# The mixer's output projection by Strassen's seven products, with its residual input on the sync queue

## The chip, the cores and the metric

The kernel runs on one core of one Trainium2 chip. The metric is the device time of one execution in microseconds (us), the median of several runs. Engines: PE (TensorE, matrix products into PSUM banks), DVE (VectorE), ACT (ScalarE), POOL (GpSimd), and SP, which here only issues DMAs. A DMA can be issued by SP, ACT or POOL; each has its own queue, and in this kernel POOL's DMAs are the ones that add to what already stands in the target.

## The reference

One layer of a decoder trunk, 512 tokens by 1024 channels, all in float32. Cut to what matters here:

```python
y_a = pool_mixer(z_pool, w_pool[i], pool_scale[i]) @ w_branch_a[i]
y_b = spatial_gating(z_uv, sgu_norm[i], w_spatial[i], b_spatial[i]) @ w_branch_b[i]
x = x + (g_a * y_a + g_b * y_b) @ w_out[i]
h = rmsnorm(x, ffn_norm[i])
x = x + conv_ffn(h, w_up[i], conv_w[i], conv_b[i], w_down[i])
x = x + gate * (p[i] @ w_ple[i])
```

The change concerns the third line, a product of 512x1024 by 1024x1024, and the loads of `x` and `p` around it.

## The kernel before

**Products.** Every float32 operand is split into a high part (a cast to float32r) and a low part (the rest), and each product is three matmuls (`mm3`, L204 to L206): high by high, high by low, low by high. A matmul covers 128 rows of contraction and 512 columns.

**Weights.** They come in tiles of 128x1024 (512 KB). A list `todo` holds, in the order of use, a pair of functions for each tile: one that issues its load on SP (`load_raw`, L81; `fetch`, L105), one that splits it (`parts`: the high part by ACT at L68, `whi`; the low part by DVE at L69, `wlo`). `take()` hands the next split tile to the products and keeps two more split ahead (`AHEAD`) and up to four loaded behind those (`LOADS`). There are four buffers of split tiles and 37 buffers (`blk`) that raw tiles and activations share. Within these limits the framework's scheduler sets the order in which each engine's instructions stand; an engine then runs its own instructions strictly in that order.

**Seven products.** `seven()` computes a product of 512 tokens by Strassen's scheme, in halves of tokens, contraction and columns, with seven products instead of eight. The weights it needs are blocks a, b, c, d and sums of them. `plan_seven` makes the sums: with `adds="some"` mostly by DVE, with `adds="all"` all of them by POOL's adding DMAs (P5: b+a; P6: the same plus c, added in place after P5's split; P7: b+c; P4: P6's sum plus d, added in place after P6's split). On the activation side `combine` and `cut_into` build D, S2, S3 and E from the two halves. P1, P2 use one pair of PSUM banks, P5, P3 another, P6, P7, P4 the pair `seeded`. Between P6 and P7 ACT copies the `seeded` pair out (`copies(0)`, L368, tiles `u`), and P7 then goes on adding in that same pair. The input projections to v and to the gates run so, and so does the down projection, in three parts, the last with `adds="all"`.

**The stage of the change.** Branch A's projection runs by token (`by_token`): for each half `fh` of the columns, four weight tiles, for each tile 24 matmuls, into four banks. After each half DVE multiplies the banks by the gate and adds branch B (L578, L579; tiles `ga`, shown as `sg`). Then the result is turned: 8 times four 128x128 transposes on PE (L617), each time into one bank, split by ACT (L236) and DVE (L237). Then the output projection, again by token: 2 halves, 4 weight tiles each, 192 matmuls, drained by DVE into `x` (L629) with squares on ACT (L607) for the next norm. Then 24 matmuls of the embedding's input (`embed`), the norm (`rstd_1`, `xn` L652), and the turning for the FFN. The tokens' rows of x are loaded by ACT's queue (L584) and the embedding's input `pt` by ACT's queue too (L590), released by markers (`later`, a one-column copy) as soon as the first half of `ga[0]` stands; `pt` is split at once (`pp`).

Of the kernel before, what the change touches and what calls it, by code (L numbers as in the profile page):

```python
# [7 lines left out]
F32 = mybir.dt.float32  # L8
# [36 lines left out]
def trunk(ctx, tc, xT, xr, pT, wsT, par, bsp, w_u0, w_u1, w_v, w_ga, w_gb, w_p, w_pl,  # L45
# [38 lines left out]
    def pairs_of(n):  # L84

        return [(q, min(2, n - q)) for q in range(0, n, 2)]

    def plan(src, cols=CW, **kw):
        got = []
        todo.append((lambda: got.append(load_raw(src)), lambda: parts(got[0], cols, **kw)))  # L90

    def plan_seven(w, order=INNER, adds="vector", spare=(), q0=0, n=HK):

# [50 lines left out]

        return [unit(prod, ch) for prod in order for ch in pairs_of(n)]

# [33 lines left out]
    for i in range(KD):  # L180
        plan(w_a[i // 4, i % 4].rearrange(flat))
    for i in range(KD):
        plan(w_o[i // 4, i % 4].rearrange(flat))
    for k in range(2):
# [162 lines left out]

    def seven(op, drain, order=INNER, fill=()):


        fill = list(fill)
        n = len(op)
        bank_of = {}
# [19 lines left out]

        for prod in order:
            b, c = ops[prod]
            if b not in bank_of:
                bank_of[b] = seeded if b == "b" else [bank() for _ in range(2)]
            o = bank_of[b]
            first = b != "b" and b not in begun
            begun.add(b)  # L380
            for ch in pairs_of(n):
                step(o, c, take(), ch, first)
                if fill:
                    fill.pop(0)()
# [25 lines left out]

    def by_token(acts, fh, banks, kps, between=None):

        for kp in kps:
            c = take()
            for b in range(NT):
                for kk in range(2):
                    k = 2 * kp + kk
                    mm3(banks[b], act(acts[k], slice(b * P, (b + 1) * P)), wslice(c, kk, T), k == 0, k == KD - 1)


# [151 lines left out]


    for fh in range(2):
# [11 lines left out]
    pp = []  # L586
# [21 lines left out]

    def columns(z, b, f):

        return z[b][:, f // HK, f % HK * P:(f % HK + 1) * P]

    def turned(z, f):

        tp = bank()
        for b in range(NT):
            PE.transpose(tp[:, b * P:(b + 1) * P], columns(z, b, f), ident)  # L617
        return tp


    m = []
    for f in range(KD):
        m.append(split(turned(ga, f)))
    xss = [small.tile([P, 2], F32, tag="xss", name="xss", bufs=NT) for _ in range(NT)]
    for fh in range(2):
        banks = [bank() for _ in range(NT)] if fh == 0 else [*seeded, bank(), bank()]
        by_token(m, fh, banks, range(KD // 2))
        for b in range(NT):
# [167 lines left out]
def _layout(i):  # L796
# [9 lines left out]
    def th(w):  # L806
        return w.reshape(KD // 2, 2, P, 2, T).transpose(3, 0, 2, 1, 4)

    def sv(w):
        return w.reshape(2, HK, P, 2, T).transpose(0, 3, 1, 2, 4).reshape(4, HK, P, T)  # L810
# [8 lines left out]
    def pairs(z):  # L819
# [21 lines left out]
        "w_b": th(a["w_branch_b"][0]),  # L841
        "w_o": th(a["w_out"][0]),
        "w_up": pairs(up),

        "w_dn": a["w_down"][0].reshape(KF // 2, 2, P, 2, T).transpose(1, 3, 0, 2, 4).reshape(4, KF // 2, P, T),
        "w_g": a["w_ple_gate"][0].reshape(KD, P, D),
# [18 lines left out]
```

## Time and profile before

| what | value |
|---|---|
| median of 3 runs | 783.2 us (782.55 to 783.73) |
| the profiled execution, its own time | 781.51 us |
| its span in the trace | 779.8 us |
| busy: PE / DVE / ACT / POOL | 768.5 / 535.3 / 373.0 / 62.7 us |
| moved by DMA | 103.2 MB, mean 132 GB/s |
| branch A's second half, the turning, the output projection | from 292.77, 314.54, 319.07 us to 362.70 us |
| the embedding's 24 matmuls, the turning for the FFN | to 368.17 and 372.73 us |

The span is what the trace covers; the execution's own time is 1.7 us more. PE's busy time counts a matmul from its start to a modelled end, so PE's rate is read from the distance between starts, not from the duration. Times inside the trace are counted from the span's start.

### The profile page before, as it was taken

What the parts mean: (1) busy time and instruction counts of PE and PEld (TensorE: products, weight loads), DVE (VectorE), ACT (ScalarE), POOL (GpSimd) and SP (SyncE); (2) the same over time, 40 slices, a digit from 0 to 9 for tenths busy, and PEclk for the clock granted to TensorE, in tenths of its full rate; (3) what the DMA queues carried; (4) which work ended last, traced back from release to release, by engine and by line L of the source; (5) the groups of instructions that cost most, each with busy time, mean ns of one, the idle gap of its engine ahead of it and who ended that gap; (6) DMA issues with size and microseconds to landing.
All of it is one profiled execution on the core that took longest, in us unless ns stands there. A gap on an engine that the chain in (4) does not pass through costs nothing.

```text
span 779.8 us, 9304 instructions
## 1 busy us (share of the span) xinstructions
PE 768.5 (99%) x3482; PEld 636.9 (82%) x3482; DVE 535.3 (69%) x752; ACT 373.0 (48%) x538; POOL 62.7 (8%) x97
## 2 busy tenths in 40 slices
PE   9999999999999999999999999999999999999996
PEld 7888888888888888888788888888888888887785
DVE  7895688866576734635576768766677776777845
ACT  6576736582232312325545454534545435457823
POOL 2310200000112100001000000000001010030300
PEclk9999999999999999999999999999999999999998
DMA  8993625124032508101832344742336572384211
GB/s 329 324 240 109 163 78 194 54 98 170 31 114 75 216 24 315 67 0 47 331 111 51 96 118 98 278 141 54 82 107 136 189 192 78 109 171 112 82 55 54
DMA packets 40926, 103.21 MB, mean 132 GB/s; under 512 B 3633, under 2 KB 3761, under 8 KB 40881
## 3 DMA queue, kind: packets, MB, share of 16 engines
q1 hardware_dynamic: 33280, 86.78, 31.8%
q0 software_dynamic: 6016, 11.54, 9.0%
q10 hardware_dynamic: 1584, 4.31, 1.6%
q8 instruction: 27, 0.44, 0.2%
q14 instruction: 19, 0.15, 0.1%
HBM read 99.46 MB, written 3.15 MB: 132 GB/s over the span
## 4 chain that ended last, share of the span: by engine, by line
PE 82%; DVE 2%; ACT 1%; issue 1%; POOL 0%; POOLq 0%; DVEq 0%; ACTq 0%
PE mm L205 22%; PE mm L206 22%; PE mm L204 22%; PE sd L204 5%; PE sd L205 5%; PE sd L206 5%; DVE wlo L69 1%; PE mm L504 1%; PE mm L617 0%; DVE xn L652 0%; POOL fr L602 0%; PE mm L680 0%; ACT whi L68 0%; ACT sq L607 0%; DVE x L629 0%
## 5 line engine op out<-in xcount | busy, mean ns | idle before, releaser
L69 DVE TENSOR_TENSOR wlo<-raw,whi 128x1024 fp32r<-128x1024 f32 (+1 forms) x186 | 218.2, 1178 | 157.1 <-ACT whi L68 156.5
L68 ACT CAST whi<-raw 128x1024 fp32r<-128x1024 f32 (+1 forms) x179 | 184.0, 1031 | 204.9 <-PE mm L206 64.4
L205 PE MATMUL mm<-blk,whi 128*128 128x512 f32 x480 | 186.8, 389 | 0.0
L204 PE MATMUL mm<-blk,whi 128*128 128x512 f32 x480 | 186.8, 390 | 0.0
L206 PE MATMUL mm<-blk,wlo 128*128 128x512 f32 x480 | 186.6, 389 | 0.0
L204 PEld LDWEIGHTS mm<-blk,whi 128*128 128x128 f32 x480 | 90.1, 188 | 19.0 <-DVE blk L240 0.2
L205 PEld LDWEIGHTS mm<-blk,whi 128*128 128x128 f32 x480 | 90.1, 188 | 18.8
L206 PEld LDWEIGHTS mm<-blk,wlo 128*128 128x128 f32 x480 | 90.1, 188 | 18.8
L204 PE MATMUL mm<-whi,blk 128*128 128x512 f32 x210 | 82.1, 391 | 0.0
L205 PE MATMUL mm<-wlo,blk 128*128 128x512 f32 x210 | 81.8, 390 | 0.0
L206 PE MATMUL mm<-whi,blk 128*128 128x512 f32 x210 | 81.7, 389 | 0.0
L204 PEld LDWEIGHTS mm<-whi,blk 128*128 128x128 f32 x210 | 39.4, 188 | 8.2 <-DVE blk L237 0.2
L206 PEld LDWEIGHTS mm<-whi,blk 128*128 128x128 f32 x210 | 39.4, 188 | 8.2
L205 PEld LDWEIGHTS mm<-wlo,blk 128*128 128x128 f32 x210 | 39.4, 188 | 8.0
L204 PE MATMUL sd<-whi,blk 128*128 128x512 f32 x114 | 44.7, 392 | 0.5 <-ACT u L368 0.5
L205 PE MATMUL sd<-wlo,blk 128*128 128x512 f32 x114 | 44.4, 389 | 0.0
L206 PE MATMUL sd<-whi,blk 128*128 128x512 f32 x114 | 44.4, 389 | 0.0
L105 POOL DMA_DIRECT2D raw<-in_w_dn x16 | 18.2, 1242 | 314.6 <-DMA raw<-in_w_dn 204.1
L204 PE MATMUL sd<-whi,cmb 128*128 128x512 f32 x92 | 36.1, 395 | 1.1 <-ACT u L368 1.1
L204 PE MATMUL mm<-whi,cmb 128*128 128x512 f32 x92 | 35.9, 390 | 0.0
L205 PE MATMUL sd<-wlo,cmb 128*128 128x512 f32 x92 | 35.8, 390 | 0.0
L206 PE MATMUL sd<-whi,cmb 128*128 128x512 f32 x92 | 35.8, 389 | 0.0
(171 smaller groups left out, 1078.7 us busy)
## 6 DMA issues: line engine op xcount, KB each, us to landing
raw<-in_w_up SPq DMA_DIRECT2D x44, 512.0 KB, 4.3
raw<-in_w_dn SPq DMA_DIRECT2D x25, 512.0 KB, 3.5
raw<-in_w_dn POOLq DMA_DIRECT2D x12, 512.0 KB, 6.0
raw<-in_w_v SPq DMA_DIRECT2D x10, 512.0 KB, 8.2
raw<-in_w_ga SPq DMA_DIRECT2D x10, 512.0 KB, 4.7
raw<-in_w_gb SPq DMA_DIRECT2D x8, 512.0 KB, 3.7
raw<-in_w_p SPq DMA_DIRECT2D x8, 512.0 KB, 4.4
raw<-in_w_b SPq DMA_DIRECT2D x8, 512.0 KB, 3.8
```

The source lines that it names most:

```text
L68: (V.tensor_copy if first else S.copy)(hi[:, :cols], raw[:, :cols])
L69: V.tensor_tensor(lo[:, :cols], raw[:, :cols], hi[:, :cols].bitcast(F32), op=ALU.subtract)
L105: (G if kw else nc.sync).dma_start(o, block_of(name, ch), **kw)
L204: PE.matmul(o, wh, ah, start=first, stop=False, **kw)
L205: PE.matmul(o, wh, al, start=False, stop=False, **kw)
L206: PE.matmul(o, wl, ah, start=False, stop=last, **kw)
L504: PE.matmul(mx[:, n * P:(n + 1) * P], vt[n].rearrange("p a t -> p (a t)")[:, f * P:(f + 1) * P], wsm[:, f, :], start=True, stop=True)
```

## The change

The output projection is done by `seven` with the order P1, P5, P2, P6, P7, P4, P3, each product in two chunks of two contraction pairs (one weight tile each, 12 matmuls). With `crossed` the first four steps are P1 chunk 0, P5 chunk 0, P1 chunk 1, P5 chunk 1. The weight's layout is the one `w_dn` has, and its sums are all made by POOL's adding DMAs. The turning is cut into four pairs (`turn_pair`): pairs 0 and 1 need only the first half of `ga` and stand inside branch A's second half, after its second and third weight tile; pairs 2 and 3 stand behind the first and second step of `seven`. A pair is 8 transposes, two copies from PSUM to tiles `s`, and the building of A11 (`a11`), D, S2, S3, E (`cmb`) and A12, A22 (`blk`). The loads of x and of `pt` go to the sync queue, released by the second half of `ga`, and `pt` is split behind the projection.

```diff
-    for i in range(KD):
-        plan(w_o[i // 4, i % 4].rearrange(flat))
+    todo.extend(plan_seven(blocks(w_o), DOWN, "all", crossed=True))
...
-        for prod in order:
+        for prod, ch in steps_of(order, n, crossed):
...
-            begun.add(b)
-            for ch in pairs_of(n):
-                step(o, c, take(), ch, first)
-                if fill:
-                    fill.pop(0)()
+            if ch[0] + ch[1] == n:
+                begun.add(b)
+            step(o, c, take(), ch, first)
+            if fill:
+                fill.pop(0)()
+            if ch[0] + ch[1] < n:
+                continue
...
+    def turn_pair(q):
+        s = []
+        for f in (2 * q, 2 * q + 1):
+            tp = turned(ga, f)
+            s.append(work("s"))
+            S.copy(s[-1], tp)
+        s1, s2 = s
+        if q % 2 == 0:
+            m11.append(block("a11", (2, 2, H), F32R))
+        t = m11[-1][:, q % 2]
+        cut_into(t, s1[:, :H])
+        z = combine(s1, s2)
+        a2 = split(s2)
+        m.append(dict(A11=t, A12=a2[:, :, :H], A22=a2[:, :, H:], **z))
+
     for fh in range(2):
         banks = [bank() for _ in range(NT)] if fh == 0 else [bank(), *seeded, bank()]
-        by_token(yp, fh, banks, range(KD // 2))
+        early = [nothing, lambda: turn_pair(0), lambda: turn_pair(1)] if fh else ()
+        by_token(yp, fh, banks, range(KD // 2), early)
...
-        later(x[b][:, 0, :1], ga[0][:, 0, :1])
-        nc.scalar.dma_start(x[b].rearrange("p a t -> p (a t)"), xr[b])
+        later(x[b][:, 0, :1], ga[b][:, 1, :1])
+        nc.sync.dma_start(x[b].rearrange("p a t -> p (a t)"), xr[b])
...
+    pt = block("pt")
     for k in range(2):
-        pt = work("pt")
-        later(pt[:, :1], ga[0][:, 0, :1])
-        nc.scalar.dma_start(pt, pT[k])
-        pp.append(act(split(pt)))
+        later(pt[:, k, :1], ga[NT - 1][:, 1, :1])
+        nc.sync.dma_start(pt[:, k], pT[k])
...
-    for f in range(KD):
-        m.append(split(turned(ga, f)))
...
-    for fh in range(2):
-        banks = [bank() for _ in range(NT)] if fh == 0 else [*seeded, bank(), bank()]
-        by_token(m, fh, banks, range(KD // 2))
-        for b in range(NT):
-            V.tensor_tensor(x[b][:, fh], banks[b], x[b][:, fh], op=ALU.add)
-            squares(b, fh, xss)
+
+    def drain_m(th, j, fh, src):
+        b = 2 * th + j
+        V.tensor_tensor(x[b][:, fh], src, x[b][:, fh], op=ALU.add)
+        squares(b, fh, xss)
+
+    seven(m, drain_m, DOWN, [lambda: turn_pair(2), lambda: turn_pair(3)], HK, crossed=True)
+    pp = [act(split(pt[:, k])) for k in range(2)]
...
-        "w_o": th(a["w_out"][0]),
+        "w_o": alt(a["w_out"][0]),
```

**The sync queue.** These are SP's DMA issues from branch A's weights (`w_a`) to the first of the FFN's (`w_up`), before:

```order
L81 DMA raw<-in_w_a 128x1024 x8
L81 DMA raw<-in_w_o 128x1024 x8
L81 DMA raw<-in_w_ple 128x1024 x2
L81 DMA raw<-in_w_up 128x1024 x5
L645 DMA ple_d<-pe 128x512 x4
```

and with the change:

```order
L81 DMA raw<-in_w_a 128x1024 x8
L112 DMA raw<-in_w_o 128x2x512 x5
L625 DMA x<-in_xr 128x1024 x4
L630 DMA pt<-in_pT 128x512 x2
L112 DMA raw<-in_w_o 128x2x512 x5
L81 DMA raw<-in_w_ple 128x1024 x2
L81 DMA raw<-in_w_up 128x1024 x5
L672 DMA ple_d<-pe 128x512 x4
```

The ten tiles of `w_o` are P1's two, P5's two and P2's first ahead of x, then P2's second, P7's two and P3's two behind x and pt. POOL issues eight adding DMAs of its own, in this order: P5 chunk 0, P6 chunk 0, P5 chunk 1, P6 chunk 1, P7 chunk 0, P4 chunk 0, P7 chunk 1, P4 chunk 1.

**ACT in the projection.** With the change, from the turning of pairs 2 and 3 to the copies after P6 (`s` from the transposes' banks; `sd` the seeded pair; the four casts in a row are those of P6's and P7's chunks, the single one behind `pt` is P4's first):

```order
L604 COPY s<-mm 128x512 x4
L337 CAST a_2654<-s 128x256
...
L242 CAST blk<-s 128x512
L68 CAST whi<-raw 128x1024
L395 COPY sd<-mm 128x512 x2
L68 CAST whi<-raw 128x1024 x4
L646 ACTIVATE sq,xss<-x 128x512 x2
L242 CAST blk<-pt 128x512
L68 CAST whi<-raw 128x1024
L374 COPY u<-sd 128x512
L242 CAST blk<-pt 128x512
L374 COPY u<-sd 128x512
```

Before, ACT had in the whole projection only a weight tile's cast for every 24 matmuls and the squares; the copies and the building of operands are new there, and the copies out of the seeded pair stand behind the casts of P7's second and P4's first tile.

**DVE at the start of the projection.** With the change, from the last of the gate's products to the low parts of A11 for pairs 2 and 3 (`a_2654`):

```order
L619 TENSOR_TENSOR sg<-mm,sg 128x512
L251 COPY x<-sg 128x1 x2
L620 TENSOR_TENSOR sg<-sg 128x512
...
L69 TENSOR_TENSOR wlo<-raw,whi 128x1024
L344 TENSOR_TENSOR d<-s 128x256
L346 TENSOR_TENSOR e<-s 128x256
L345 TENSOR_TENSOR d<-d,s 128x256
L347 TENSOR_TENSOR e<-s,d 128x256
L344 TENSOR_TENSOR d<-s 128x256
...
L338 TENSOR_TENSOR a_2654<-s,a_2654 128x256
L338 TENSOR_TENSOR cmb<-d,cmb 128x2x256
L338 TENSOR_TENSOR cmb<-e,cmb 128x2x256
L243 TENSOR_TENSOR blk<-s,blk 128x512
L338 TENSOR_TENSOR a_2654<-s,a_2654 128x256
```

Pair 3's sums stand ahead of pair 2's A11, and pair 3's A11 behind all the rest of pair 2; before, DVE went from the gate straight to eight low parts (L237), one for each turned block.

## Rows read from the trace of the kernel before

**Rows 1.** The page: busy time by engine, granted clock by fortieths, last chain by engine.

```profile
PE 768.5 (99%) x3482; PEld 636.9 (82%) x3482; DVE 535.3 (69%) x752; ACT 373.0 (48%) x538; POOL 62.7 (8%) x97
PE 82%; DVE 2%; ACT 1%; issue 1%; POOL 0%; POOLq 0%; DVEq 0%; ACTq 0%
```

**Rows 2.** Stages: start:end, us, PE, PEld, DVE, ACT, POOL busy, clock, DMA, GB/s.

```profile
319.07:362.70 43.63, 43.63 (x193) 36.15 (x193) 16.84 (x23) 11.99 (x21) 0.55 (x1) 1.00 0.00 1
362.70:368.17 5.47, 5.47 (x25) 4.46 (x24) 4.88 (x14) 4.27 (x9) 1.65 (x3) 1.00 0.25 96
```

**Rows 3.** Timeline of PE at the turning: start, us, instruction, [idle before <-releaser].

```profile
314.54 2.47 PE L617 MATMUL mm<-ident,sg 128*128 128x128 f32 x20
317.28 1.85 PE L617 MATMUL mm<-ident,sg 128*128 128x128 f32 x12 [0.27 <-DVE blk L237]
319.07 0.50 PE L204 MATMUL mm<-whi,blk 128*128 128x512 f32 x1
319.41 0.40 PE L205 MATMUL mm<-wlo,blk 128*128 128x512 f32 x1
```

**Rows 4.** Timeline of DVE there: the gate's last product and sums.

```profile
314.74 0.69 DVE L578 TENSOR_TENSOR sg<-mm,sg 128x512 f32<-128x512 f32 x1
315.34 1.28 DVE L579 TENSOR_TENSOR sg<-sg 128x512 f32<-128x512 f32 x2
```

**Rows 5.** Groups of DVE and ACT: count | busy us, mean ns | idle before.

```profile
L69 DVE TENSOR_TENSOR wlo<-raw,whi 128x1024 fp32r<-128x1024 f32 x171 | 208.2, 1222 | 153.3 <-ACT whi L68 152.9
L338 DVE TENSOR_TENSOR d<-cc 128x256 f32<-128x256 f32 x11 | 4.7, 425 | 0.4
L68 ACT CAST whi<-raw 128x1024 fp32r<-128x1024 f32 x171 | 179.2, 1050 | 203.4 <-PE mm L206 64.0 <-PE mm L205 51.3 <-issue 38.4
L387 ACT COPY sd<-mm 128x512 f32<-128x512 f32 x12 | 6.9, 575 | 2.6 <-PE mm L206 2.6
L607 ACT ACTIVATE sq<-x 128x512 f32<-128x512 f32 x16 | 10.0, 626 | 10.8 <-DVE x L629 5.2 <-DVE x L669 5.1 <-issue 0.5
```

**Rows 6.** DMA issues of the span: queue, count, KB each, median us to landing.

```profile
raw<-in_w_dn SPq DMA_DIRECT2D x25, 512.0 KB, 3.5
raw<-in_w_dn POOLq DMA_DIRECT2D x12, 512.0 KB, 6.0
raw<-in_w_v POOLq DMA_DIRECT2D x4, 512.0 KB, 13.2
```

**Rows 7.** DMA of 262 to 266 us, SP's queue alone.

```profile
DMA packets 463, 1.69 MB, mean 422 GB/s; under 512 B 51, under 2 KB 51, under 8 KB 463
```

**Rows 8.** DMA queues of 37 to 47 us: packets, MB, share (q0 POOL's, q1 SP's).

```profile
q0 software_dynamic: 679, 1.30, 69.9%
q1 hardware_dynamic: 683, 1.33, 39.9%
```

**Rows 9.** DMA queues of 690 to 697 us.

```profile
q0 software_dynamic: 392, 0.74, 64.8%
q1 hardware_dynamic: 277, 1.01, 40.0%
```

**Rows 10.** Timeline of POOL: three adding DMAs issued in a row.

```profile
690.01 3.06 POOL L105 DMA_DIRECT2D raw<-in_w_dn  x3 [3.28 <-DVE wlo L69]
```

**Rows 11.** PE's waits: total us, times, longest.

```profile
PE sd L204 <- ACT u L368: 1.6, 2, 1.1
```

**Rows 12.** Timeline of PE: its first instructions and its last.

```profile
1.13 3.70 PE L261 MATMUL wake<-ones 128*128 128x128 f32 x18 [1.13 <-DVE neghalf L265]
...
772.30 0.28 PE L206 MATMUL mm<-whi,xe 128*128 128x256 f32 x1
```

**Rows 13.** Stages behind PE's last instruction, columns as in rows 2.

```profile
774.00:775.00 1.00, 0.00 (x0) 0.00 (x0) 0.58 (x2) 0.51 (x2) 0.14 (x1) 1.00 0.00 0
775.00:776.00 1.00, 0.00 (x0) 0.00 (x0) 0.48 (x1) 0.57 (x1) 0.40 (x1) 0.78 0.00 0
776.00:777.00 1.00, 0.00 (x0) 0.00 (x0) 0.00 (x0) 0.16 (x1) 0.00 (x0) 0.50 0.20 80
```

**Rows 14.** Timeline of POOL and DVE at the norm behind the projection.

```profile
366.62 1.10 POOL L602 TENSOR_TENSOR fr<-fms,neghalf 128x1 f32<-128x1 f32 x2 [2.38 <-DVE fms L600]
...
367.20 1.67 DVE L652 TENSOR_SCALAR xn<-x,fr 128x512 f32<-128x512 f32 x4 [0.52 <-POOL fr L602]
```

More of the change, by code (lines that the diff above doesn't have):

```diff
@@ L86, in pairs_of, with steps_of @@
         return [(q, min(2, n - q)) for q in range(0, n, 2)]
+    def steps_of(order, n, crossed=False):
+        steps = [(prod, ch) for prod in order for ch in pairs_of(n)]
+        if crossed:
+            steps[1], steps[2] = steps[2], steps[1]
+        return steps
     def plan(src, cols=CW, **kw):
@@ L90, in plan, with plan_seven @@
         todo.append((lambda: got.append(load_raw(src)), lambda: parts(got[0], cols, **kw)))
-    def plan_seven(w, order=INNER, adds="vector", spare=(), q0=0, n=HK):
+    def plan_seven(w, order=INNER, adds="vector", spare=(), q0=0, n=HK, crossed=False):
         raw = {}
@@ L143, in unit @@
             return load, cut
-        return [unit(prod, ch) for prod in order for ch in pairs_of(n)]
+        return [unit(prod, ch) for prod, ch in steps_of(order, n, crossed)]
     def prepare(loads=LOADS):
@@ L346, in trunk, with seven @@
            "P2": ("a", "A12"), "P3": ("c", "E")}
-    def seven(op, drain, order=INNER, fill=()):
+    def seven(op, drain, order=INNER, fill=(), n=None, crossed=False):
         fill = list(fill)
-        n = len(op)
+        n = n or len(op)
         bank_of = {}
@@ L409, in nothing, with by_token @@
         pass
-    def by_token(acts, fh, banks, kps, between=None):
+    def by_token(acts, fh, banks, kps, after=()):
+        after = list(after)
         for kp in kps:
@@ L418, in by_token @@
                     mm3(banks[b], act(acts[k], slice(b * P, (b + 1) * P)), wslice(c, kk, T), k == 0, k == KD - 1)
+            if after:
+                after.pop(0)()
     x2 = []
@@ L571, in trunk, with columns, turned @@
             group_maps(i // 5)
+    def columns(z, b, f):
+        return z[b][:, f // HK, f % HK * P:(f % HK + 1) * P]
+    def turned(z, f):
+        tp = bank()
+        for b in range(NT):
+            PE.transpose(tp[:, b * P:(b + 1) * P], columns(z, b, f), ident)
+        return tp
+    m = []
+    m11 = []
+    def turn_pair(q):
[12 more added lines that the diff above has]
+        m.append(dict(A11=t, A12=a2[:, :, :H], A22=a2[:, :, H:], **z))
     for fh in range(2):
         banks = [bank() for _ in range(NT)] if fh == 0 else [bank(), *seeded, bank()]
-        by_token(yp, fh, banks, range(KD // 2))
+        early = [nothing, lambda: turn_pair(0), lambda: turn_pair(1)] if fh else ()
+        by_token(yp, fh, banks, range(KD // 2), early)
         for b in range(NT):
@@ L607, in squares @@
         S.activation(sq, x[b][:, fh], AF.Square, accum_out=sums[b][:, fh:fh + 1])
[L609 to L615, printed above, removed]
-        for b in range(NT):
-            PE.transpose(tp[:, b * P:(b + 1) * P], columns(z, b, f), ident)
-        return tp
-    m = []
-    for f in range(KD):
-        m.append(split(turned(ga, f)))
-    xss = [small.tile([P, 2], F32, tag="xss", name="xss", bufs=NT) for _ in range(NT)]
-    for fh in range(2):
-        banks = [bank() for _ in range(NT)] if fh == 0 else [*seeded, bank(), bank()]
-        by_token(m, fh, banks, range(KD // 2))
-        for b in range(NT):
-            V.tensor_tensor(x[b][:, fh], banks[b], x[b][:, fh], op=ALU.add)
-            squares(b, fh, xss)
+    xss = [small.tile([P, 2], F32, tag="xss", name="xss", bufs=NT) for _ in range(NT)]
+    def drain_m(th, j, fh, src):
[4 more added lines that the diff above has]
+    pp = [act(split(pt[:, k])) for k in range(2)]
     c_ple = [take(), take()]
@@ L807, in th, with alt @@
         return w.reshape(KD // 2, 2, P, 2, T).transpose(3, 0, 2, 1, 4)
+    def alt(w):
+        n = w.shape[0] // P // 2
+        return w.reshape(n, 2, P, 2, T).transpose(1, 3, 0, 2, 4).reshape(4, n, P, T)
     def sv(w):
@@ L841, in _layout @@
         "w_b": th(a["w_branch_b"][0]),
-        "w_o": th(a["w_out"][0]),
+        "w_o": alt(a["w_out"][0]),
         "w_up": pairs(up),
-        "w_dn": a["w_down"][0].reshape(KF // 2, 2, P, 2, T).transpose(1, 3, 0, 2, 4).reshape(4, KF // 2, P, T),
+        "w_dn": alt(a["w_down"][0]),
         "w_g": a["w_ple_gate"][0].reshape(KD, P, D),
```

1 line of the change is left out of this document (removed).

## The prediction

> **What bounds the kernel now.** I read the page first: PE is busy for 99% of the span and 82% of the last chain are matmuls [rows 1]. So PE's order is the clock of the kernel, and a change is worth the matmuls it removes less the gaps it opens. Then the stages: the output projection takes 43.63 us for its 192 matmuls with a matmul always running, clock 1.00, and moves no data (1 GB/s); 0.227 us a matmul. The 24 of the embedding behind it take 5.47 us [rows 2]. Third, PE's timeline at the turning: 32 transposes from 314.54 to 319.07 us with one gap of 0.27 us, the only wait there [rows 3]. In the whole trace the waits for the copies out of the seeded banks, which every seven-product stage has, come to 1.6 us [rows 11]. The reader is to see a stage in which nothing waits: the weights lie there long before, and DVE and ACT have time over. All the change can gain is matmuls, all it can lose is in hand-overs that don't exist yet.
>
> **The change part by part.** T is the start of P1's first matmul.
>
> *Matmuls.* 7 products x 4 contraction pairs x 2 banks x 3 = 168 instead of 192: -24 x 0.227 = **-5.45 us**, all on PE's path. The transposes stay 32. Going from transposes back to matmuls costs 0.34 instead of 0.227 us between the first two starts [rows 3], 0.11 more; that happens once before and five times after: **+0.45**.
>
> *Operands for P1's second chunk.* Pairs 0 and 1 are turned 11 and 5 us ahead of T, in a stage where ACT and DVE keep up; I cost them at nothing, and if that cover is gone their price is the same kind as that of pairs 2 and 3. These two come late. Before, the gate's last sum ends at 316.62, 2.1 us after PE would go on [rows 3, 4]. Now pair 1's three low parts stand among the gate's instructions (0.60 each, since two take 1.28 [rows 4]): T+4.1 with the markers. Two weight splits of 1.22 [rows 5]: T+6.6. Pair 2's four sums (0.425 each, overlapping a little [rows 5]): T+8.1. In PE, two steps of 12 (2.73 each) and 16 transposes (0.13 each) would bring P1's second chunk at T+7.8, but P1 and P5 hold four of the five unseeded banks, so a pair's second four transposes wait for the ACT copy (0.58 [rows 5]) of the first four: pair 3's copies end at T+9.1. DVE's order then has pair 3's four sums (T+10.7), pair 2's A11 (T+11.1), three low parts, pair 3's A11 (T+13.3). The third matmul of the chunk wants the first of these at T+9.0, the sixth the second at T+11.9: 2.1 + 1.4, with 0.7 for the bank and 0.5 for pair 0's and 1's D behind the gate **4.7, less the old 0.27: +4.4**. Ends: 1.1 (A11 straight behind the copies) and 6.2 (no overlap between DVE's instructions).
>
> *P7.* Without other waits P6 ends at T + 8 x 2.73 + 16 x 0.13 + 0.3 + 4.7 = T+28.9. P7 adds into the seeded banks, so it must wait for the copies out of them, and these stand on ACT behind the casts of P7's second and P4's first tile (the order shown above). So P7 waits for two adding DMAs. Their way: x's first marker is copied at T+3.5, and SP issues x, pt, P2's second tile and P7's two after it, 8 tiles' worth. A tile alone lands 3.5 us after issue [rows 6], of which 1.25 is moving (0.524 MB at 422 GB/s [rows 7]): P2's second tile at T+13.2, P7's at T+14.5 and 15.7, all 2.7 later because P6's second sum is added meanwhile. P2's tile is cast on ACT at T+15.9; then two seeded copies, P6's first cast (T+19.2), its low part on DVE (T+20.4). Only then may POOL issue P4's first addition, and P7's second behind it, 1.02 later [rows 10]: T+21.4. P7's first was issued at T+17.3. An addition alone lands after 6.0 us [rows 6]. In traffic POOL's queue moved 1.30 MB in 10 us at a share of 69.9% [rows 8], so 0.186 MB/us alone, 2.8 us a tile, and 3.2 us are fixed, some 2.2 of them ahead. SP's queue is full then (P3's tiles, `w_ple` and five of `w_up`, nine tiles that wait for nothing), and in turn with such loads POOL's queue moved 0.74 MB in 7 us, 4.9 us a tile [rows 9]; beside loads like `w_o`'s 1.30 MB in 10, 4.0 a tile [rows 8]. Three additions in line from T+19.5: landed at T+35.2 by rows 9, 32.5 by rows 8, 28.9 alone. ACT then has P7's cast, two squares, half of pt, P4's cast and a copy: 1.05 + 1.26 + 0.6 (taken as such a copy) + 1.05 + 0.58 = 4.5 [rows 5]. P7 starts at T+39.7, 37.0 or 33.4: a wait of 10.8, 8.1 or 4.5 us. The queue holds mostly `w_up`-like tiles then, so I stay near rows 9: **+10.0**, ends 4.5 and 13 (each addition as slow as `w_v`'s 13.2 [rows 6]: T+21.4 + 13.2 + 4.5 is 10.2, and the P2 tile 3 us later by the same slowness).
>
> By the Trainium skill (DMA: Bandwidth & Descriptors, section Anatomy of one DMA — SWDGE (gpsimd) path) a DMA from GpSimd takes about 2.0 us plus its bytes at 436 GB/s, 3.2 us for a tile; with an estimate from that the wait would be some 0.6 us and the kernel end near 785. The trace disagrees: 6.0 us for an addition alone, 13.2 beside loads [rows 6].
>
> *Clock.* PE's last matmul ends at 772.58, and the granted clock falls from 1.00 to 0.50 (2.4 to 1.2 GHz) within 775 to 776 us, at 775.56 if 0.78 is the mean [rows 12, 13]: about 3 us after. A wait of 10 us is longer. What the way back costs shows only at the start, where 18 matmuls of 128 columns took 3.70 us, 0.21 each [rows 12], against 0.12 for transposes of that size (2.47 for 20 [rows 3]): some 3 us at the lower level. Half of them lost: **+1.5**, ends 0 and 3.
>
> *The end.* P3's result goes through two subtractions and two additions (0.6 each), a square with its read-out (0.8), two small ones, two powers on POOL (1.10) and four scalings (1.67) [rows 4, 5, 14], 7.0 us with the hand-overs, behind 5.47 us of the embedding [rows 2], so PE idles before the FFN's turning, which it didn't: **+1.5**, ends 0 and 2.8. pt's split stands in the middle of ACT's order and is counted at P7.
>
> *Nothing* for: x's transfer (it lands before P2's drain), ACT's queue without its six DMA issues (their issuing is not on PE's path now), POOL's powers (behind the eight additions, which are issued 20 us earlier). More `w_o` traffic, 4 MB of additions, costs only where it meets P7.
>
> Sum: -5.45 + 0.45 + 4.4 + 10.0 + 1.5 + 1.5 = **+12.4**. The profiled execution took 781.5 us, so 793.9 by its own time; the median of the runs is 1.7 higher, 783.2, and the forecast against it is **795.6 us**.
>
> **The rivals.**
> - *Additions in quiet queues.* If POOL's queue gets what it gets alone, the wait is 4.5 us and the clock hardly falls (0.4): +5.8, **789.0**. For it: isolated landings [rows 6]. Against it: nine tiles lie in SP's queue at that moment. The page of the Trainium skill named above (DMA: Bandwidth & Descriptors) points this way, and further.
> - *The cover holds, faster.* The mechanism is P7's second tile: if it is cast before T+24.4, 4.5 us ahead of P6's end, the copies are on time and P7 doesn't wait. That needs it landed 11 us earlier than I find. With the operands at their lower end and the end covered: -5.45 + 0.45 + 1.1 = -3.9, **779.3**. For it: the down projection's last part makes its sums in the same way and waited at most 1.1 us [rows 11]. Against it: there nothing like x stands ahead of the tiles on SP.
> - *Slower still.* If each addition takes `w_v`'s 13.2 us and the upper ends of the other terms hold, 13 + 6.2 + 3 + 2.8 - 5.0: +20, **803**.
> - *No difference.* If P7 waits no more than 0.7 us, the clock stays and the operands and the end cost what I find, the 24 matmuls are just used up: +0.9, **784**. That needs the additions some 9 us earlier than rows 9 give [rows 9].
>
> **How the numbers follow.** Forecast 0.63; quiet queues 0.18; slower still 0.08; faster 0.07; no difference 0.04. About 0.2% (1.6 us) is what a measurement of this kernel can tell from no change. Slower by more: 0.63 + 0.18 + 0.08 = 0.89; same 0.04; faster 0.07. The forecast alone, with P7's wait from 7 to 12, runs from 791 to 799. The range takes in the quiet queues and leaves out the other three, 0.19: **787 to 800**.
>
> **What would show it.** Right: 24 matmuls fewer; PE idle once for 8 to 11 us before a seeded matmul, put down to ACT's copy `u`, with the granted clock at 0.50 behind it; ACT at that time idle until a raw tile of `w_o` lands; gaps of 1 to 2 us in P1's second chunk, put down to DVE's or ACT's `a11`. Wrong: additions that land within 6 us of issue while SP's queue is full; `u` copied right at P6's end; or x landing so early that `w_o`'s second half isn't late.

## The result and the profile after

The changed kernel takes **802.6 us** (median of 4 runs, 800.79 to 802.97), the kernel before 782.9 in the same comparison: a ratio of 1.0249, 95% interval 1.0237 to 1.0261. The direction was as forecast and so was the place; the size was not: 795.6 was forecast, and the range ended at 800. The profiled execution took 802.72 us with a span of 801.0, so 21.2 us more than the one before, where the forecast had 12.4.

The page of the changed kernel: PE's work and the share of matmuls in the last chain [rows 1].

```profile
PE 768.5 (96%) x3458; PEld 634.7 (79%) x3458; DVE 554.0 (69%) x786; ACT 389.9 (49%) x566; POOL 72.6 (9%) x105
PE 51%; DVE 2%; ACT 1%; issue 1%; POOL 0%; POOLq 0%; DVEq 0%; ACTq 0%
```

There are 24 matmuls fewer, yet PE's busy time is what it was, 768.5 us: some of what is left runs slower. PE's share of the last chain has gone from 82 to 51%, because the chain, followed back from the last instruction, now ends at ACT's copy `u` at 362.29 us: what lies before it is not in these shares.

The stages (start:end, us, busy time and count of PE, PEld, DVE, ACT, POOL, granted clock, DMA share, GB/s) from P1's first matmul at T = 317.26 to P6's end, from there to P7, P7's first matmuls, and the turning for the FFN behind the embedding [rows 2]:

```profile
317.26:347.99 30.73, 25.69 (x113) 19.15 (x111) 17.91 (x35) 12.02 (x19) 6.08 (x5) 1.00 0.86 284
347.99:362.82 14.83, 0.15 (x1) 0.00 (x0) 5.00 (x8) 5.31 (x10) 0.00 (x0) 0.61 0.81 192
362.82:368.39 5.57, 5.57 (x13) 4.40 (x14) 2.56 (x3) 1.90 (x3) 0.00 (x0) 0.50 0.00 0
...
387.30:394.07 6.77, 4.67 (x34) 3.32 (x32) 6.19 (x15) 5.79 (x10) 1.10 (x2) 1.00 0.84 305
```

The first row is four products (P1, P5, P2, P6) and 16 transposes at full clock, with 5 us of gaps. The second is nothing but a wait. In the third, matmuls take nearly twice their time, at a granted clock of 0.50, the lower of the two levels. In the last, 32 transposes that took 4.56 us before (368.17 to 372.73) take 6.77.

PE's waits (total us, times, longest). Of these, the kernel before had only the first kind, at 1.6 us in all [rows 11], and 0.27 us for `blk` at the turning [rows 3]:

```profile
PE sd L210 <- ACT u L374: 16.3, 3, 14.7
PE mm L212 <- DVE a L338: 1.8, 2, 1.0
PE mm L210 <- ACT sd L395: 1.2, 1, 1.2
...
PE mm L593 <- DVE xn L679: 1.1, 1, 1.1
PE mm L593 <- DVE blk L246: 1.0, 1, 1.0
PE mm L210 <- ACT a L337: 1.0, 1, 1.0
```

PE's timeline in the projection, its gaps alone [rows 3], and the first matmuls behind the long one (start, us, instruction, idle before and its releaser):

```profile
321.17 0.50 PE L210 MATMUL mm<-whi,cmb 128*128 128x512 f32 x1 [0.16 <-DVE x L251]
...
325.96 0.66 PE L593 MATMUL mm<-ident,sg 128*128 128x128 f32 x4 [0.73 <-ACT s L604]
...
327.60 0.50 PE L210 MATMUL mm<-whi,a 128*128 128x512 f32 x1 [0.98 <-ACT a L337]
...
329.22 0.50 PE L212 MATMUL mm<-whi,a 128*128 128x512 f32 x1 [0.89 <-DVE a L338]
...
331.36 0.50 PE L212 MATMUL mm<-whi,a 128*128 128x512 f32 x1 [0.95 <-DVE a L338]
...
336.97 0.50 PE L210 MATMUL mm<-whi,blk 128*128 128x512 f32 x1 [1.23 <-ACT sd L395]
...
362.82 0.79 PE L210 MATMUL sd<-whi,cmb 128*128 128x512 f32 x1 [14.68 <-ACT u L374]
363.42 0.63 PE L211 MATMUL sd<-wlo,cmb 128*128 128x512 f32 x1
363.84 0.63 PE L212 MATMUL sd<-whi,cmb 128*128 128x512 f32 x1
```

A matmul follows the last by 0.42 us here, by 0.227 elsewhere.

Why P7 waits stands in ACT's timeline. `u` are the copies that P7 waits for; the casts at 337.32 are P6's two, at 348.35 and 358.56 P7's two, at 361.25 P4's first:

```profile
335.38 1.05 ACT L68 CAST whi<-raw 128x1024 fp32r<-128x1024 f32 x1 [4.41 <-DMA raw<-in_w_o]
336.33 1.06 ACT L395 COPY sd<-mm 128x512 f32<-128x512 f32 x2
337.32 2.00 ACT L68 CAST whi<-raw 128x1024 fp32r<-128x1024 f32 x2
348.35 1.04 ACT L68 CAST whi<-raw 128x1024 fp32r<-128x1024 f32 x1 [9.02 <-DMA raw<-in_w_o]
358.56 1.04 ACT L68 CAST whi<-raw 128x1024 fp32r<-128x1024 f32 x1 [9.17 <-DMA raw<-in_w_o]
...
361.25 1.04 ACT L68 CAST whi<-raw 128x1024 fp32r<-128x1024 f32 x1
362.20 0.57 ACT L374 COPY u<-sd 128x512 f32<-128x512 f32 x1
```

P6 ended at 348.14 (362.82 less 14.68). ACT stood still for 9 us, twice, for tiles of `w_o` that were not summed yet, with the copies queued behind; the pair it was to copy out lay ready all that time from 348.1 on. POOL's timeline shows when those additions were issued, P7's first at 338.43, then P4's first and P7's second with one more [rows 10]:

```profile
338.43 1.20 POOL L112 DMA_DIRECT2D raw<-in_w_o  x1 [13.89 <-DMA raw<-in_w_o]
339.93 3.68 POOL L112 DMA_DIRECT2D raw<-in_w_o  x3 [0.30 <-DVE wlo L69]
```

The first waited for its base tile (a DMA on SP's queue), not for POOL. And this is what the DMA queues carried then (packets, MB, share; q0 POOL's, q1 SP's): first from 338.5 to 342.7 us, where no q0 stands at all, then from 344 to 352 us [rows 8, 9].

```profile
q1 hardware_dynamic: 578, 1.74, 103.3%
...
q0 software_dynamic: 428, 0.84, 56.8%
q1 hardware_dynamic: 424, 1.54, 51.5%
```

So an addition issued at 338.43 moved nothing for some 4.2 us, and then the two queues moved as many packets each: 428 against 424. At 0.84 MB in 8 us a tile of 0.524 MB takes 5.0 us.

### The profile page after: what moved, and what is told of

Same layout as the page of the kernel before. It is cut to its first block, busy times and chain, and to the rows that moved or that the text cites. A ratio compares the mean times of both kernels' runs of the same rounds, so it can differ in the third digit from the quotient of the medians.

```text
span 801.0 us, 9355 instructions
## 1 busy us (share of the span) xinstructions
PE 768.5 (96%) x3458; PEld 634.7 (79%) x3458; DVE 554.0 (69%) x786; ACT 389.9 (49%) x566; POOL 72.6 (9%) x105
## 4 chain that ended last, share of the span: by engine, by line
PE 51%; DVE 2%; ACT 1%; issue 1%; POOL 0%; POOLq 0%; DVEq 0%; ACTq 0%
PE mm L211 14%; PE mm L212 14%; PE mm L210 14%; PE sd L210 3%; PE sd L212 2%; PE sd L211 2%; DVE wlo L69 1%; DVE xn L679 0%; POOL fr L641 0%; PE mm L707 0%; ACT whi L68 0%; PE mm L593 0%; ACT sq L646 0%; DVE u L378 0%; DVE fms L639 0%
## 5 line engine op out<-in xcount | busy, mean ns | idle before, releaser
L69 DVE TENSOR_TENSOR wlo<-raw,whi 128x1024 fp32r<-128x1024 f32 (+1 forms) x192 | 225.4, 1180 | 164.7 <-ACT whi L68 164.2
L68 ACT CAST whi<-raw 128x1024 fp32r<-128x1024 f32 (+1 forms) x185 | 190.1, 1031 | 213.2 <-PE mm L211 52.1
L210 PE MATMUL mm<-whi,blk 128*128 128x512 f32 x170 | 66.7, 392 | 1.2 <-ACT sd L395 1.2
L211 PE MATMUL mm<-wlo,blk 128*128 128x512 f32 x170 | 66.3, 390 | 0.0
L212 PE MATMUL mm<-whi,blk 128*128 128x512 f32 x170 | 66.2, 389 | 0.0
L210 PE MATMUL sd<-whi,cmb 128*128 128x512 f32 x108 | 43.6, 405 | 15.8 <-ACT u L374 15.8
L112 POOL DMA_DIRECT2D raw<-in_w_dn x16 | 18.1, 1238 | 314.6 <-DMA raw<-in_w_dn 204.4
L211 PE MATMUL sd<-wlo,cmb 128*128 128x512 f32 x108 | 43.0, 398 | 0.0
L212 PE MATMUL sd<-whi,cmb 128*128 128x512 f32 x108 | 43.0, 398 | 0.0
L210 PE MATMUL mm<-whi,cmb 128*128 128x512 f32 x108 | 42.3, 392 | 0.3 <-DVE x L251 0.2
L211 PE MATMUL mm<-wlo,cmb 128*128 128x512 f32 x108 | 42.1, 390 | 0.0
L210 PE MATMUL sd<-whi,blk 128*128 128x512 f32 x106 | 41.6, 393 | 0.5 <-ACT u L374 0.5
L212 PE MATMUL mm<-whi,cmb 128*128 128x512 f32 x108 | 42.0, 389 | 0.0
L211 PE MATMUL sd<-wlo,blk 128*128 128x512 f32 x106 | 41.3, 389 | 0.0
L212 PE MATMUL sd<-whi,blk 128*128 128x512 f32 x106 | 41.3, 389 | 0.0
L210 PEld LDWEIGHTS mm<-whi,blk 128*128 128x128 f32 x170 | 31.9, 188 | 8.1 <-ACT sd L395 1.7
```

The source lines that it names most:

```text
L68: (V.tensor_copy if first else S.copy)(hi[:, :cols], raw[:, :cols])
L69: V.tensor_tensor(lo[:, :cols], raw[:, :cols], hi[:, :cols].bitcast(F32), op=ALU.subtract)
L112: (G if kw else nc.sync).dma_start(o, block_of(name, ch), **kw)
L210: PE.matmul(o, wh, ah, start=first, stop=False, **kw)
L211: PE.matmul(o, wh, al, start=False, stop=False, **kw)
L212: PE.matmul(o, wl, ah, start=False, stop=last, **kw)
```

## The experiments

The theory: P7 waits for two adding DMAs, which start late because their base tiles stand behind x on the sync queue, and are slow because that queue is full of loads; ACT's order turns the lateness of P7's second tile into a wait of its first; the clock's fall comes on top. The rivals are named with each run. All times are medians beside runs of the kernel before on the same chip (783.2 us for the first four runs, 782.2 for the next four, 782.6 for the last two; the changed kernel's 802.6 stood beside 782.9). What a run takes off the change is the difference of the medians; by the distances to before it is 12.2 instead of 12.9 us in run 5 and 6.0 instead of 6.7 in run 6. Line numbers in the runs are up to 12 higher than with the change.

**1. x off the sync queue.**

```diff
     for b in range(NT):
-        later(x[b][:, 0, :1], ga[b][:, 1, :1])
-        nc.sync.dma_start(x[b].rearrange("p a t -> p (a t)"), xr[b])
+        later(x[b][:, 0, :1], ga[0][:, 0, :1])
+        nc.scalar.dma_start(x[b].rearrange("p a t -> p (a t)"), xr[b])
...
-        later(pt[:, k, :1], ga[NT - 1][:, 1, :1])
-        nc.sync.dma_start(pt[:, k], pT[k])
+        later(pt[:, k, :1], ga[0][:, 0, :1])
+        nc.scalar.dma_start(pt[:, k], pT[k])
```

> The changed kernel, with the loads of x and of the embedding's input on ACT's queue again, released by the first half of the gate, so that nothing of them stands ahead of the second half of w_o on the sync queue. Theory (P7 waits for two adding DMAs that are begun late because their base tiles stand behind x, and that are slowed by the sync queue's loads): P2's second tile and P7's base tiles land some 3 to 4 us earlier, P7's wait falls from 14.7 to about 11 us, 798.5 us (797 to 800). Rival A (the place in the sync queue does not matter, the additions are slow wherever they start, since the same bytes move): 801.5 to 803. Rival B (the place in the queue is all): the wait falls by the 6 loads' time, 2 MB at 422 GB/s and the additions met by them, 7 us or more: 795 or less.

Measured: **797.2 us** (ratio to before 1.0172, interval 1.0157 to 1.0188), 5.4 less than with the whole change. P7's wait fell to 12.23 us, and P2's wait of 1.2 is gone.

```profile
357.66 0.80 PE L210 MATMUL sd<-whi,cmb 128*128 128x512 f32 x1 [12.23 <-ACT u L374]
```

The place in the sync queue counts, but it is the smaller part: rival A falls, and rival B. The scheduler also ordered other work anew: POOL has P4's first addition ahead of P7's first, and ACT the copies and casts for P1's second chunk in another order. So the 5.4 us are not shown to be the queue's place alone: 2.45 are P7's wait, 1.23 P2's, and where the rest comes from was not separated.

**2. The loads behind held back.**

```diff
+        if hold:
+            later(raw[:, :1], held[0][0][:, :1].bitcast(F32))
         nc.sync.dma_start(raw[:, :n], src)
```

`hold` is set for the first tile of `w_ple`, and `held[0]` is the split of P4's first tile.

> The changed kernel, with the first load of w_ple, and with it all that stands behind it on the sync queue (w_ple's second tile and five tiles of w_up), held back by a marker until P4's first tile has been cast. P3's tiles still go ahead. Theory: the additions for P7 and P4 then have the queues for themselves: instead of 9.9 us for P7's first and 5.0 us for each behind it, about 6 us and 2.8 to 3.5 us each; P7's wait falls from 14.7 to 6 or 8 us, 794 to 797 us. Rival A (the sync queue's loads do not slow the additions, they are that slow by themselves when three stand in line): no change, 801.5 to 803. Rival B (the late start by the place in the queue is all): the same no change.

Measured: **793.8 us** (1.0129, 1.0113 to 1.0144), 8.8 less. From 344 to 352 us POOL's queue is alone:

```profile
q0 software_dynamic: 797, 1.54, 106.5%
```

1.54 MB in 8 us is 2.7 us a tile, where beside SP's loads it was 5.0. P7's first addition, issued at 338.60, was seen by ACT at 345.44, 6.8 us later instead of 9.9, and P7's second 5.1 us behind it instead of 10.2. From 338.6 to 341 us, behind its issue, there is still no q0:

```profile
338.60 1.20 POOL L116 DMA_DIRECT2D raw<-in_w_o  x1 [13.52 <-DMA raw<-in_w_o]
...
q1 hardware_dynamic: 416, 0.99, 105.2%
```

P7's wait is then

```profile
354.32 0.80 PE L222 MATMUL sd<-whi,cmb 128*128 128x512 f32 x1 [5.91 <-ACT u L386]
```

The contention is the larger part, and both rivals fall.

**3. No adding DMAs.**

```diff
-    todo.extend(plan_seven(blocks(w_o), DOWN, "all", crossed=True))
+    todo.extend(plan_seven(blocks(w_o), DOWN, "vector", crossed=True))
```

> The changed kernel, with all sums of w_o made by DVE in place (adds=vector, as the gate's second projection has it) and no adding DMA; the sync queue then loads 8 tiles of w_o instead of 10. Theory: P7's wait is gone, and with it the clock's fall: 802.6 - 14.7 - 2.7 = 785 us (784 to 787), and what is left against before, +2, is the operands of P1's second chunk, the switches and the end less the 24 matmuls. Rival A (DVE becomes the bound: 8 sums of 1.2 us more on it): 788 to 792, with waits of PE for DVE's wlo. Rival B (P7 waits for something else than additions, since ACT's copies stand behind the casts anyway): 792 to 797, P7's wait 5 to 9 us.

Measured: **784.1 us** (1.0015, 1.0005 to 1.0026). P7 doesn't wait, the clock of the profiled execution doesn't fall, and DVE takes the eight sums without PE waiting for a weight in the projection. What the additions cost in the change is thus 18.5 us, and all the rest of it, seven products with their operands and their end, is worth +0.8 us. Even these hold some clock: the two executions with a mean granted clock of 0.998 took 782.8 and 783.1 us, the eight with 0.993 to 0.996 took 783.8 to 785.9.

**4. PE kept busy in the wait.** The copies of P6's pair are followed by matmuls that nobody reads:

```diff
+    def keep_warm(w):
+        o = pst.tile([P, T], F32, tag="st", name="warm")
+        for _ in range(60):
+            PE.matmul(o, w[1][:, :P], w[0][:, :T], start=True, stop=True)
```

> The changed kernel, with 60 matmuls of 128x512 that nobody reads between P6 and P7 (into a bank of its own, from P6's last weight tile): 60 x 0.227 = 13.6 us, just less than P7's wait of 14.7. They lengthen nothing, and PE does not stand still. Theory (the 12 matmuls at 0.43 instead of 0.227 us behind the wait are the granted clock at half, because PE stood still): the clock stays at 1.00, the time falls by 12 to 13 x 0.2 = 2.5 to 2.7 us, 800 us. Rival (the matmuls behind the wait are slow for another reason, such as the weights' arrival): they are as slow as before and the time stays 802 to 803.

Measured: **799.4 us** (1.0205, 1.0184 to 1.0226), 3.2 less. The stages there, the idle matmuls and then P7's first chunk:

```profile
347.40:361.79 14.39, 13.99 (x63) 11.26 (x61) 5.01 (x8) 5.13 (x10) 0.00 (x0) 1.00 0.85 214
361.79:364.51 2.72, 2.72 (x12) 2.24 (x13) 2.12 (x3) 1.90 (x3) 0.00 (x0) 1.00 0.03 6
```

P7's 12 matmuls take 2.72 us at clock 1.00; at 0.50 these and the start of a thirteenth took 5.57. That 60 matmuls more make a kernel faster is the clock's price, shown: some 2.6 us by the trace. The medians have 3.2; P7 also started 0.7 us earlier, counted from P1's start, which the edit does not explain.

**5. Both causes of the lateness taken away.** The edits of runs 1 and 2 together.

> Both of the earlier edits on the changed kernel together: x and the embedding's input on ACT's queue, and w_ple and w_up held back until P4's first tile has been cast. This is the prediction's rival of the quiet queues made real. Theory (the late start and the sync queue's loads are two causes that overlap: the first alone took 5.4 us off 802.6, the second alone 8.8): the additions start at about T+18, nothing runs beside them, three in line take 6 + 2.6 + 2.6 = 11.2 us by the landings of the run that held the loads back, and ACT's casts, squares and copies behind them 3 to 4.5 us; P7 starts at about T+33 to 35, its wait is 4.5 to 6.5 us, and the time 789 to 791 us. Rival A (the two add up): 802.6 - 5.4 - 8.8 = 788.4 or less. Rival B (the additions' own time is the floor already reached by holding back alone): 793 to 794.

Measured: **789.7 us** (1.0096, 1.0080 to 1.0111), 12.9 less.

```profile
349.92 0.79 PE L222 MATMUL sd<-whi,cmb 128*128 128x512 f32 x1 [4.66 <-ACT u L386]
```

This is the prediction's rival of the quiet queues with its condition made true: it said a wait of 4.5 us and 789.0, and found are 4.66 and 789.7. The wait is the rival's; that the time is so near is in part luck. Against before it is +7.5 in this round, not +5.8, and the clock, which the rival put at 0.4, cost some 2.1: 11 matmuls in 4.75 us from 349.92 instead of 2.61. The two causes overlap (5.4 and 8.8, together 12.9), and what stays is the additions' own time, three in line (P4's first, here as in run 1, ahead of P7's), and ACT's line behind them.

**6. ACT's order.** DVE casts P7's second and P4's tiles.

```diff
-                o = parts(z, cols, spare=prod in spare)
+                mine = crossed and (prod == "P4" or prod == "P7" and ch[0] > 0)
+                o = parts(z, cols, first=mine, spare=prod in spare)
```

> The changed kernel, with the high parts of P7's second tile and of both of P4's tiles cast by DVE instead of ACT, so that ACT's copies u no longer stand behind casts that wait for the second and third addition. All DMAs stay. Theory (the wait of 14.7 us is for the additions, but half of it is paid only because the copies stand in line behind P7's second and P4's first tile): P7 starts when its first tile and the copies are done, some 10 us earlier at about 353 us of the trace, and then waits again, for its second tile (landed at 358.5, cast and split by DVE at about 361): two waits of 4 to 6 us each instead of one of 14.7, 795 to 798 us. Rival A (ACT's order costs nothing, since P7's second tile is needed anyway): 801 to 803. Rival B (ACT's order is all of it, the tiles are there): 788 to 790.

Measured: **795.9 us** (1.0179, 1.0165 to 1.0193), 6.7 less, with all DMAs as they were. The time is the expected one, the second wait isn't:

```profile
353.62 0.79 PE L211 MATMUL sd<-whi,cmb 128*128 128x512 f32 x1 [6.05 <-ACT u L375]
...
359.88 0.50 PE L212 MATMUL sd<-wlo,cmb 128*128 128x512 f32 x1 [0.35 <-DVE wlo L69]
```

After a wait of 6.05 us P7's first chunk runs at half clock, and so slowly reaches almost to the second tile. So the order on ACT alone cost 8.6 us of the wait and some 6 of the time; a first tile that had been there since 348 was worth nothing while the copies stood behind the second. Part of the 6.05 us is still ACT's order: P7's first tile was split at 350.04, and the copies came at 352.99, behind two squares that waited for DVE's drain, and the casts of `pt`.

**7. The loads moved in the kernel before.** x and `pt` on the sync queue as in the change, the projection by token as before.

```diff
-        later(x[b][:, 0, :1], ga[0][:, 0, :1])
-        nc.scalar.dma_start(x[b].rearrange("p a t -> p (a t)"), xr[b])
+        later(x[b][:, 0, :1], ga[b][:, 1, :1])
+        nc.sync.dma_start(x[b].rearrange("p a t -> p (a t)"), xr[b])
...
+    pp = [act(split(pt[:, k])) for k in range(2)]
```

> The kernel before, with the other part of the change alone: the loads of x and of the embedding's input on the sync queue, released by the second half of the gate, and the input's split behind the projection. The projection stays by token, its weights without additions. Theory (moving the loads costs only what stands behind them late on the queue; here the last three tiles of w_o are plain loads, wanted 27 us later): no change, 783 to 785 us. Rival (x itself is late: the drain of the projection or the turning waits for it or for the queue): 787 us or more.

Measured: **784.8 us** (1.0029, 1.0018 to 1.0039), 2.5 more than before, at the upper end of what was expected and not "no change". Nothing waits for x. PE's turning waits for the gate:

```profile
318.52 0.33 PE L615 MATMUL mm<-ident,sg 128*128 128x128 f32 x1 [1.00 <-DVE sg L579]
319.43 1.85 PE L615 MATMUL mm<-ident,sg 128*128 128x128 f32 x12 [0.58 <-DVE blk L237]
```

against 0.27 us [rows 3]. DVE's timeline shows what lies there, a weight's low part and markers between the gate's last product and its last sum, where before the two last sums stood right behind it [rows 4]:

```profile
315.99 0.68 DVE L578 TENSOR_TENSOR sg<-mm,sg 128x512 f32<-128x512 f32 x1
316.59 0.14 DVE L245 COPY x<-sg 128x1 f32<-128x1 f32 x1
316.65 1.21 DVE L69 TENSOR_TENSOR wlo<-raw,whi 128x1024 fp32r<-128x1024 f32 x1
317.78 0.68 DVE L579 TENSOR_TENSOR sg<-sg 128x512 f32<-128x512 f32 x1
```

No instruction waits for the moved transfers, but with their markers the order changed on the engine that PE was about to wait for. The gaps are 1.3 us of the 2.5; where the rest comes from this run does not settle.

**8 to 10. A version that is faster.** Run 3 leaves the operands of P1's second chunk and the end. Run 8 takes run 3's kernel with P4 drained last; run 9 turns pairs 0 and 1 one weight tile earlier; run 10 also releases x and `pt` by the first half of the gate.

```diff
+OUT = ('P1', 'P5', 'P6', 'P7', 'P3', 'P2', 'P4')
...
-    todo.extend(plan_seven(blocks(w_o), DOWN, "all", crossed=True))
+    todo.extend(plan_seven(blocks(w_o), OUT, "vector", crossed=True))
...
-    seven(m, drain_m, DOWN, [lambda: turn_pair(2), lambda: turn_pair(3)], HK, crossed=True)
+    seven(m, drain_m, OUT, [lambda: turn_pair(2), lambda: turn_pair(3)], HK, crossed=True)
...
-        early = [nothing, lambda: turn_pair(0), lambda: turn_pair(1)] if fh else ()
+        early = [lambda: turn_pair(0), lambda: turn_pair(1)] if fh else ()
...
-        later(x[b][:, 0, :1], ga[b][:, 1, :1])
+        later(x[b][:, 0, :1], ga[0][:, 0, :1])
...
-        later(pt[:, k, :1], ga[NT - 1][:, 1, :1])
+        later(pt[:, k, :1], ga[0][:, 0, :1])
```

> The changed kernel with all sums of w_o by DVE, as in the run that had no adding DMA (784.1 us against 783.2 before in that round), and the products in the order P1, P5, P6, P7, P3, P2, P4, so that the last product drained is P4, whose banks go into x by one addition each, and P3's subtractions and additions are done during P2 and P4. Theory (P3's long drain at the end cost two gaps of 1.1 and 1.0 us before the FFN's turning, and P1's copies are covered by P5's second chunk as well as by P2): both gaps go, 0 to 1 us is lost at P6, 782 us (781.3 to 783): the first form that is not slower than the kernel before, by 0.1 to 0.2%. Rival A (the end waits for the norm's chain however P3 is placed): 784. Rival B (P6 now waits for the copies into the seeded pair): 785 to 787.

Measured for run 8: **783.1 us** (1.0002, 0.9991 to 1.0012), 780.6 to 784.9 over 11 runs, so wider than the others. The gaps of 1.1 and 1.0 us at the end have shrunk to one of 0.24:

```profile
371.05 1.98 PE L594 MATMUL mm<-ident,xn 128*128 128x128 f32 x12 [0.24 <-DVE blk L247]
```

The gaps at the end behaved as expected, the median is 1 us above what was expected and just outside the range. The five runs with a mean granted clock of 0.997 or 0.998 took 780.6 to 782.0 us, the six with 0.993 to 0.996 took 783.1 to 784.9.

> The kernel of the last run (sums of w_o by DVE, P4 drained last), with one edit more: the turning of pairs 0 and 1 stands behind branch A's first and second weight tile of the second half instead of behind the second and third, so that DVE's low parts of pair 1 are done before the gate's last products. Theory (the term of the operands: P1's second chunk is late by what stands on DVE between the gate and A11, and pair 1's share of that is some 1.5 us): the gaps in P1's second chunk fall from 3.6 us by 1.5 to 2, and the time from 783.1 to about 781.3 (780.5 to 782), below the kernel before. Rival A (the chain through transposes, ACT's copies and A11 of pairs 2 and 3 sets it, whatever stands on DVE before): 782.5 to 783.5. Rival B (the first pair is turned too early, before the first half of the gate stands, and PE waits in branch A): 784 or more.

Measured for run 9: **780.1 us** (0.9959, 0.9946 to 0.9973), 0.4 us below the expected range. In P1's second chunk only two gaps are left:

```profile
324.47 0.66 PE L594 MATMUL mm<-ident,sg 128*128 128x128 f32 x4 [0.73 <-ACT s L605]
...
326.16 0.50 PE L211 MATMUL mm<-whi,a 128*128 128x512 f32 x1 [1.03 <-ACT a L338]
```

and in the stage behind them the clock is at half for 3.3 us:

```profile
326.84:330.14 3.30, 3.30 (x9) 2.58 (x8) 3.30 (x8) 1.13 (x3) 0.00 (x0) 0.52 1.05 372
```

That is the likely reason for the scatter of runs 3 and 8, whose gaps were as large or larger; their own profiles caught executions without it, so it is not shown there.

> The same as the run with pairs 0 and 1 turned earlier, and x and the embedding's input released by the first half of the gate's first tile, still on the sync queue, so that the six one-column markers leave DVE's order behind the gate and no load waits for the gate's end. Theory (the markers and the gate's end cost part of the operands' gaps, as the run of the kernel before with the loads moved cost 2.5 us in the same place): another 0.5 to 1.5 us, 780 us (779.3 to 781), 0.3% faster than before. Rival (the markers are too short to matter): as without this edit, 781 to 782.

Measured for run 10: **778.7 us** (0.9946, 0.9934 to 0.9958), faster than both kernels, and again below the expected range. Its largest gap from the gate to the FFN is a wait for a weight's low part, once P1's operands no longer hold PE up:

```profile
336.13 0.50 PE L212 MATMUL sd<-wlo,cmb 128*128 128x512 f32 x1 [1.49 <-DVE wlo L70]
```

Against before it is 3.9 us less, where the 24 matmuls alone are worth 5.45.

## Why the prediction was right, and where it failed

The mechanism held: PE idle once before a seeded matmul, put down to ACT's `u`, ACT idle for raw tiles of `w_o`, the clock at half behind it, gaps in P1's second chunk, a longer end. The sizes, term by term against the profiled executions:

| term | forecast | found | from |
|---|---|---|---|
| 24 matmuls | -5.45 | -5.45 | the page |
| switches | +0.45 | +0.5 | 0.34 between the first two starts, as before |
| P1's second chunk | +4.4 | +3.4 | gaps of 0.16, 0.73, 0.98, 0.89, 0.95 less the old 0.27 |
| P2 | nothing | +1.2 | the wait for `sd` L395 |
| P7's wait | +10.0 | +14.7 | the timeline |
| clock | +1.5 | +2.6 | 13 matmuls in 5.66 us from 362.82 instead of 3.06 |
| end | +1.5 | +2.1 | the waits for `xn` and `blk` |
| hand-overs under the profile's gaps | nothing | +1.3 | what is left: the stage's 78.6 us less before's 58.2 and less the rows above |
| ahead of the stage | nothing | +1.0 | branch A's end |
| sum | +12.4 | +21.3 | measured: 21.2 |

The stage is counted from branch A's end to the FFN's first matmul: 314.54 to 372.73 before; 317.26 to 394.07 after, and 1.75 us for the 16 transposes that now stand in branch A. The 1.0 us ahead of it is no effect of the change: between kernels that are alike up to there, P1's start differed by 0.9 us from run to run. The hand-overs come of how gaps are counted, from a matmul's modelled end: P2's first matmul started 1.39 us later than the distance of 0.227 would have it, and its gap shows as 1.23.

**The step that failed is P7's wait**: 4.7 of the 8.9 us by which the sum was short, and without them 797.9 us would have lain inside the range. In it two prices failed, both of the additions' start and not of their rate:

| | forecast | found |
|---|---|---|
| P2's second tile cast | T+15.9 | T+18.1 |
| P7's first addition issued | T+17.3 | T+21.2 |
| it begins to move | T+19.5 | T+25.4 |
| first landed, as seen by ACT | T+25.4 | T+31.1 |
| third landed, as seen by ACT | T+35.2 | T+41.3 |
| P7 starts | T+39.7 | T+45.6 |
| P6 ends | T+28.9 | T+30.9 |

First, "of which 1.25 is moving": P2's and P7's base tiles were priced as if SP's queue had 422 GB/s for itself, with 2.7 us for the addition under way. From 323.3 to 334 us, while that addition was under way, the queue and the addition's landing stand so:

```profile
q1 hardware_dynamic: 995, 2.76, 73.9%
...
raw<-in_w_o POOLq DMA_DIRECT2D x1, 512.0 KB, 10.7
```

SP's queue moved 2.76 MB in 10.7 us, 258 GB/s instead of 422. The addition's share, some 2.8 us of the engines' time, was priced rightly; in its own 73.9% SP's queue had 349 GB/s. Also x was issued at T+4.0 instead of T+3.5. So P7's first addition was issued 3.9 us later than forecast. Second, "3.2 us are fixed, some 2.2 of them ahead": taken from an addition alone, and the part ahead found to be some 4.2 us with SP's queue full, 2.0 more. P6 ended 2.0 us later than forecast too, which takes so much off the wait. From the first landing to the third it is 10.2 us for two, 5.1 each, where rows 9 gave 4.9 [rows 9], and from there to P7 4.3 us where 4.5 were forecast; those prices were right. The time ahead of the first packet was again 4.2 us in run 1, whose SP queue is as full (issued at 336.35, no packet until 340.6). In runs 2 and 5, with the loads held back, it was 2.4 and 1.8 us (338.60 to 341.0, 336.19 to 338.0), and the first packets came as SP's queue ran out. So the lateness goes with a full queue; what in the queue causes it stays open.

P2's wait comes of the same lateness: P2 needs the bank pair that ACT copies to the seeded one, and these copies stand behind the cast of P2's second tile. The text had that very order ("P2's tile is cast on ACT at T+15.9; then two seeded copies") and used it for P7 only. By its own times the copies would end at some T+18.0, when P5 ends too, so the term had no slack, and a tile 2.2 us late made a wait of 1.2. The clock was priced at half of some 3 us at the lower level; the lower level held for 5.6 us, and run 4 shows the price.

The rivals: the quiet queues had the right wait and the wrong condition, and a clock priced too low (run 5). "Slower still" has the measured time, 803, but not by its way: the operands and the end stayed below its ends, and the wait and the clock passed or came close to theirs. The times of "no difference" (784) and "faster" (779.3) are met only when the additions are gone (run 3 and, with more edits, run 10); with the additions the nearest is run 5's 789.7. For waits on x itself "nothing" was right, for its markers it wasn't quite (run 7), and what x costs as load ahead of the tiles of `w_o` is in P2's and P7's terms (run 1).

By the Trainium skill (DMA: Bandwidth & Descriptors, section Anatomy of one DMA — SWDGE (gpsimd) path), a tile takes an estimated 3.2 us from GpSimd. The runs disagree for additions: 2.7 us a tile of moving alone, 5.0 beside loads, and ahead of the first packet 1.8 to 2.4 us with the loads held back and 4.2 beside them.

## What to carry to other kernels

A DMA that adds is not priced by its landing time alone: count what must land first, when its first packet goes beside a full queue, and what a full queue leaves of its rate, here about half; where another engine has time for the sums, as DVE had here (run 3), make them there. On an engine that runs in order, work that is ready must not stand behind work that waits for a transfer: here 8.6 us of a 14.7 us wait were that order, and some 6 us of the time. And a change that removes matmuls pays first for every gap it opens, then for the clock behind the gap; close the gaps before counting the gain.

## What was not expected of the hardware

- POOL's and SP's queues shared the engines by packets, one to one (428 and 424 in 8 us, as 679 and 683 before [rows 8]), so additions fell from 797 packets in 8 us alone to 428, and SP's loads moved 1.54 MB in these 8 us, 192 GB/s, where alone they had 1.74 MB in 4.2.
- After waits of 4.66, 5.91, 6.05, 12.23 and 14.68 us PE came back at half clock, each time for 3.5 to 6 us, 8 to 13 matmuls at 0.42 instead of 0.227, 1.5 to 2.6 us lost: in these five runs the price does not go with the wait's length. Two gaps of 0.73 and 1.03 us did it once (run 9); the changed kernel's gaps of up to 1.23 us ahead of P6 did not.
